# Hybrid SSD and attention block: shorter inverse roots, block 11 staged from the last scan row, slabs for the second norm taken late, a ring of 16

## The chip, the cores and the metric

One core of a Trainium2 chip runs the kernel. The engines by the names of the profile: PE multiplies matrices, DVE (vector), ACT (scalar) and POOL (GpSimd) work on tiles in on-chip memory, SP issues all transfers of this kernel, in the order of its program. The metric is the device time of one execution in microseconds, median of the runs.

## The reference, cut to what matters

The input is 1024 tokens of 1024 channels in float32. All of the following is computed once (depth 1):

```python
def rmsnorm(x, g):
    y = xf * lax.rsqrt(jnp.mean(xf * xf, axis=-1, keepdims=True) + EPS)
    return (y * g.astype(jnp.float32)).astype(x.dtype)
...
h = rmsnorm(x, norm_mix[l])
proj = h @ w_in[l]
z, xBC, dt_raw, qkv, gate_logits = jnp.split(proj, offs[1:], axis=-1)
y_ssm = mamba2_branch(z, xBC, dt_raw, ...) @ w_ssm_out[l]     # scan in chunks of 128, then a norm by 4 groups of 512 channels
y_att = dilated_attention_branch(q, k, v) ... @ w_att_out[l]  # 12 heads in 3 windows and dilations
mixed = gates[:, :, 0] * y_ssm + gates[:, :, 1] * y_att
x = x + mixed @ w_mix_out[l]
h = rmsnorm(x, norm_ffn[l])
x = x + (jax.nn.silu(h @ w_ffn_gate[l]) * (h @ w_ffn_up[l])) @ w_ffn_down[l]
return rmsnorm(x, norm_final)
```

There are thus four kinds of inverse root: the first norm, the norm of the scan's output by groups, the norm ahead of the feed-forward part (the second norm), and the final norm.

## The kernel before, in words

**Arithmetic.** Every float32 operand is split into a high and a low part, and a product is three matmuls (`mm3`). The large products go by a seven-product scheme: matrices are cut into 2 x 2 blocks, seven products of sums of blocks are formed, and added up. For the product with `w_ssm_out` the seven products have the numbers 1 to 7 and the order `SSM_ORDER` = 1, 2, 3, 6, 5, 7, 4.

**Order.** The program's order is made as the kernel is built. The matmuls are written in a main sequence; all other work is written as tasks, generators that yield what they wait for: a time, a tile, or the name of an event. A planner (`Pace`) advances a modelled clock with each matmul and runs the tasks whose conditions have come about by that clock, by priority. In `Pace.note` the model has a lag of 2.0 us for a transfer behind another transfer, dropped before the event `heads`. On the chip each engine, and SP too, works through its instructions in that order and waits on semaphores.

**Slabs.** On-chip memory is cut into slabs. `Store.room` hands them out in the order in which tasks asked, one line for all; a task that is refused waits, and those behind it wait as well.

**Inverse roots.** An inverse root is done by DVE on a tiny tile, from an integer estimate and three Newton steps. `rsqrt_steps` has 11 operations after the mean, each fed by the one before. It is called by `stat_task` (three groups of tokens in the first norm), `quarter_task` (four groups of channels in the scan) and `mo_task` (two halves of tokens, second norm). The final norm has its own form, `inverse_root`, of 14 operations, one of which (`sq`, half the argument) hangs beside the chain; `out_half` calls it for groups of 4, 1 and 3 blocks of 128 tokens. What follows is a scaling of the rows and the output transfers, six of them in the last group.

**Stages.** First norm; the projections with the scan and the attention heads as background; then the merge, in which the scan's output, scaled by rows and channels, is multiplied by `w_ssm_out`. `block_load` stages blocks of the scan's output: "11" and "21" before the merge in slabs, "12" and "22" in it in the places called `yb`; `block_task` scales them (POOL by rows, ACT by channels), `y_splits` splits them into pieces of the ring (`N_RING` slabs, 8 used by each product), `block_sums` forms the differences. Block "11" and "21" both wait for the event `heads` (the last attention head). The scan's row factors go out to `rs_d`, the last of them at the event `ssd3`.

**Attention in the merge.** `att_ops(th)` loads the attention's output of half `th` of the tokens from `att_d`, in two parts of two loads each, and splits each part: raw, high and low, three slabs while it lasts. Half 0 is asked for at product 5, half 1 in product 4, the last. `att_unit` multiplies by `w_att_out`, `x2_task` loads x anew (four loads of 512 KB for each half) and `mix_unit` multiplies by `w_mix_out`.

**Slabs held from the merge on.** 37 slabs are there at the merge. 8 hold weights, 14 the ring, 2 the gates (`gslabs`), 1 the second norm's weights (`nf`); the rest serves blocks 11 and 21, the sums (`cblk`) and `att_ops`.

Of the kernel before, what the change touches and what calls it, by code (L numbers as in the profile page):

```python
# [13 lines left out]
I32 = mybir.dt.int32  # L14
AF = mybir.ActivationFunctionType
ALU = mybir.AluOpType
# [4 lines left out]
P = 128  # L21
S = 1024
D = 1024
# [9 lines left out]
EPS = 1e-6  # L33
# [23 lines left out]
N_WTS = 7  # L57
N_WTS_B = 6
N_WTS_M = 8
N_RING = 14  # L60
N_BRIDGE = 3
N_FLAT_GATES = 4
N_SSD = 6
# [124 lines left out]
class Pace:  # L188
# [38 lines left out]
    def note(self, kind, op, aps, args, kw):  # L227
        c = self.cost(kind, op, aps, args, kw)
        outs = [_key(aps[0])] + ([_key(kw["accum_out"])] if "accum_out" in kw else [])
        ins = [_key(a) for a in aps[1:]]  # L230
        s = 0.0
        for k in ins + outs:
            t, by = self.wr.get(k, (0.0, kind))
            if by != kind or (kind == "dma" and k in ins):
                s = max(s, t)
            elif kind != "pe":
                s = max(s, t - (2.0 if kind == "dma" and "heads" in self.events else 0.025))
        for k in outs:
            t, by = self.rd.get(k, (0.0, kind))
            if by != kind:  # L240
                s = max(s, t)
        if kind == "pe":
            self.stall += max(0.0, s - self.t)
            e = self.t = max(self.t, s) + c
            lag = 0.1
        else:
            s = max(self.eng[kind], s)
            if kind == "pool" or kind == "dve" and all(_space(a) != PSUM for a in aps):
                s = self.take_port(s, c, kind)
            e = self.eng[kind] = s + c  # L250
            lag = 2.0 if kind == "dma" else 0.15
        for k in outs:
            self.wr[k] = (e + lag, kind)
        for k in ins:
            if e >= self.rd.get(k, (0.0, ""))[0]:
                self.rd[k] = (e, kind)
# [82 lines left out]
def hybrid_block(ctx, tc, x, norm_mix, w_in, b_gate, conv_w, conv_b, dt_bias, a_log, d_skip, ssm_norm,  # L339
                 w_ssm_out, w_att_out, w_mix_out, norm_ffn, w_ffn_gate, w_ffn_up, w_ffn_down, norm_final,  # L340
                 consts, rope, out):
    pace = Pace()
    nc = Core(tc.nc, pace)
# [13 lines left out]
    slabs = Store([Slot(cpool, f"slab{i}", 1024) for i in range(N_SLAB)])  # L357
# [79 lines left out]
        return w[k0 * P:(k0 + nk) * P, c0:c0 + nc_].rearrange("(k p) c -> p k c", p=P)  # L437

    def rsqrt_steps(r, v, t):
        nc.vector.tensor_scalar(t.bitcast(I32), v.bitcast(I32), 1, None, ALU.logical_shift_right)  # L440
        yield [t]
        nc.vector.tensor_scalar(r.bitcast(I32), t.bitcast(I32), -1.0, 1597463007.0, ALU.mult, ALU.add)
        yield [r]
        for _ in range(3):
            nc.vector.scalar_tensor_tensor(t, r, -0.5, r, ALU.mult, ALU.mult)
            yield [t]
            nc.vector.tensor_tensor(t, t, v, ALU.mult)
            yield [t]
            nc.vector.scalar_tensor_tensor(r, t, 1.5, r, ALU.add, ALU.mult)
            yield [r]  # L450

    def rsqrt(r, v, t):
        for _ in rsqrt_steps(r, v, t):
# [2 lines left out]
    def small(tag, w):  # L456
        return kpool.tile([P, w], F32, tag=f"{tag}{w}", name=f"{tag}{w}_{nid()}", bufs=4)
# [1247 lines left out]
    def block_load(name):  # L1705
        kh, th = BLOCKS[name]
        for i in range(4):
            kk = kh * 4 + i
            yield f"ssd{kk // 2}"
            early = name in ("11", "21")  # L1710
            if early:
                yield "heads"
                yield from spare(2)
            else:
                yield 3.0
            if kk % 2 == 0:
                yield from scale_rows(kk // 2, th, slabs if early else halves)
            if early:
                yield from slabs.room()
                blk[name].append(slabs.get([P, 2, 512]))  # L1720
            fetch_y(blk[name][i], kk, th)
            pace.fire(f"f{name}{i}")
# [65 lines left out]
    def att_ops(th):  # L1788
        ts_ = slice(th * 512, (th + 1) * 512)
        for q in range(2):  # L1790
            for i in range(2):
                yield f"sl{q * 2 + i}"
            yield from slabs.room()
            raw = slabs.get([P, 2, 512])
            for i in range(2):
                nc.sync.dma_start(raw.v[:, i, :], att_d[q * 2 + i][:, ts_])
            ysp[th, q] = yield from split_piece(raw, slabs)
            raw.free()
            pace.fire(f"ya{th}{q}")
# [44 lines left out]
    fplans = [[plan(cols_of(w, 0, KD, f * P, P), KD) for w in (w_ffn_gate, w_ffn_up)] for f in range(N_DIRECT)]  # L1844
    wstate["limit"] = len(loads)

    nf = slabs.get([P, D])
    nc.sync.dma_start(nf.v, norm_ffn[0].partition_broadcast(P))
    x2t, gst, ssq, merged, cblk, pb = {}, {}, {}, {}, {}, {}
    h2 = {"hi": [None, None], "lo": [None, None]}  # L1850

# [70 lines left out]
    def mo_task(th, cb, outs, done):  # L1922
        yield f"x2{th}"
        if cb == 0:
            ssq[th] = kpool.tile([P, 4, 2], F32, tag="ssq", name=f"ssq{th}", bufs=2)
        cs = slice(cb * 512, (cb + 1) * 512)
        for j in range(4):
            xv = x2t[th, j].v[:, cs]
            yield [outs[j], x2t[th, j]]
            nc.vector.scalar_tensor_tensor(xv, outs[j], 0.5, xv, ALU.mult, ALU.add)  # L1930
            if (j + 1) % (4 // len(done)) == 0:
                done[(j + 1) * len(done) // 4 - 1].free()
        yield from halves.room()
        junk = halves.get([P, 512])
        for j in range(4):
            t0 = th * 512 + j * P
            yield [x2t[th, j]]
            nc.sync.dma_start(x2_d[t0:t0 + P, cs], x2t[th, j].v[:, cs])
            nc.scalar.activation(junk.v, x2t[th, j].v[:, cs], AF.Square, accum_out=ssq[th][:, j, cb:cb + 1])
        junk.free()  # L1940
        if cb == 0:
            return
        for n in ("hi", "lo"):
            h2[n][th] = hp.tile([P, KD, 512], F32R, tag=f"h{n}{th}", name=f"h2{n}{th}")
        yield [ssq[th]]
        rv, rs, rt = small("rv", 4), small("rs", 4), small("rt", 4)
        nc.vector.tensor_reduce(rv, ssq[th], AX.X, ALU.add)
        nc.vector.tensor_scalar(rv, rv, 1.0 / D, EPS, ALU.mult, ALU.add)
        rsqrt(rs, rv, rt)
        raw = None  # L1950
        if th == 1:
            for n in ("T3", "T2"):
                yield from F.t_slabs(n)
            raw = F.T["T3"], F.T["T2"]
        for j in range(4):
            xj = x2t[th, j].v
            yield max(0.0, pace.rd[_key(xj)][0] - pace.t)
            nc.vector.scalar_tensor_tensor(xj, xj, rs[:, j:j + 1], nf.v, ALU.mult, ALU.mult)
            yield [xj]
            yield from split_tokens(xj, h2["hi"][th], h2["lo"][th], j * P, raw)  # L1960
            x2t[th, j].free()
            pace.fire(f"h2_{th}{j}")
        if th == 1:
            nf.free()
            slabs.pieces.extend(gslabs.pieces)

    def two_holders(t):
# [94 lines left out]
            then(kp)  # L2062
        pace.spawn(mo_task(th, cb, outs, held), 0.3, -1)

    gslabs = Store([slabs.pieces.popleft() for _ in range(2)])
    pace.fire("merge")
    for u in gates:
        u()
    for name, tag in (("T2", "hhi0"), ("12", "hlo0"), ("22", "hhi1"), ("C", "hlo1")):
        t = hp.tile([P, 4, 2, 512], F32, tag=tag, name=f"yb{name}")  # L2070
# [4 lines left out]
    for i, p in enumerate(SSM_ORDER):  # L2075
        if p == 5:
            pace.spawn(att_ops(0), 0.0, 1)
        if p == 7:
            pace.spawn(merged_place(0), 0.0, -1)
            for o in range(KD):  # L2080
                pace.spawn(gate_load(0, o))
        if p == 4:
            def then(j):
                if j == 1:
                    pace.spawn(att_ops(1), 0.0, 1)
                for o in (2 * j, 2 * j + 1):
                    att_unit(0, o)
            ssm_product(p, i % 2, then)
        else:
            ssm_product(p, i % 2)  # L2090
# [209 lines left out]

    sums = {}

    def inverse_root(v, r, t, h, sq):
        nc.vector.tensor_tensor(v, sq[:, :, 0], sq[:, :, 1], ALU.add)
        yield v
        nc.vector.tensor_scalar(v, v, EPS, None, ALU.add)
        yield v
        nc.vector.tensor_scalar(t.bitcast(I32), v.bitcast(I32), 1, None, ALU.logical_shift_right)
        nc.vector.tensor_scalar(h, v, -0.5, None, ALU.mult)
        yield t  # L2310
        nc.vector.tensor_scalar(r.bitcast(I32), t.bitcast(I32), -1.0, 1597463007.0, ALU.mult, ALU.add)
        yield r
        for _ in range(3):
            nc.vector.tensor_tensor(t, r, h, ALU.mult)
            yield t
            nc.vector.tensor_tensor(t, t, r, ALU.mult)
            yield t
            nc.vector.scalar_tensor_tensor(r, t, 1.5, r, ALU.add, ALU.mult)
            yield r

    def out_half(jj, b):

# [4 lines left out]
        s = sums[group]  # L2327
# [6 lines left out]
        s[1] -= 1  # L2334
        if s[1]:
            return
        v, r, t, h = (small(k, 4)[:, :n] for k in ("rv", "rs", "rt", "sq"))
        yield [s[0]]
        for w in inverse_root(v, r, t, h, s[0]):
            if jj < 4:  # L2340
                yield [w]
        for i in range(n):
# [79 lines left out]
```

## Time and profile before

| what | us |
|---|---|
| median of 3 runs | 2153.78 (2153.51 to 2153.95) |
| profiled execution | 2149.6 |
| its span | 2147.8 |
| PE busy | 2103.4 (98% of the span) |
| DVE busy | 1617.8 (75%) |
| ACT busy | 937.4 (44%) |
| POOL busy | 695.5 (32%) |

The profile shows one execution on the chip. The span runs from its first to its last instruction; the execution's time holds a little more around it. Busy time of PE is counted with modelled ends. The granted clock of the core is 0.994 of full speed on the mean.

### The profile page before, as it was taken

To read this page: it belongs to the slowest core of one execution; us is meant where nothing else is said; L and a number is where in the kernel's file an instruction comes from. 1 tells how busy PE (TensorE), PEld (TensorE's weight loads), DVE (VectorE), ACT (ScalarE), POOL (GpSimd) and SP (SyncE) were. 2 spreads that over 40 slices of the span, in tenths; PEclk is the share of its full clock that TensorE was granted. 3 is DMA by queue.
4 is the path that set the end of the run, shared out by engine and by line. 5 is a ranking of instruction groups with operands and counts; after the bars stand their busy time and mean duration, and the time that the engine had idled before them with its cause. 6 is when DMAs were issued, how large, how long until landed. Compare 5 with 4: busy or idle time off the path is not lost. (4 is left out here: it accounts for less than half of the span.)

```text
span 2147.8 us, 27780 instructions
## 1 busy us (share of the span) xinstructions
PE 2103.4 (98%) x10236; PEld 1736.2 (81%) x10236; DVE 1617.8 (75%) x2130; ACT 937.4 (44%) x1686; POOL 695.5 (32%) x440
## 2 busy tenths in 40 slices
PE   6999999999999999999999999999999999999997
PEld 6788888878888788878888788888878888888886
DVE  5687988877775678789784677766787777757787
ACT  4543443444434465545554543333533232324444
POOL 1333234343332445455444410002254444420102
PEclk9999999999999999999999999999999999999999
DMA  4533346655555465667548743764142323349333
GB/s 130 161 106 104 103 133 186 186 167 167 180 168 196 152 193 191 193 221 231 171 130 263 252 143 113 237 233 143 30 137 84 123 89 118 108 157 340 116 94 117
DMA packets 317707, 341.77 MB, mean 159 GB/s; under 512 B 21316, under 2 KB 251652, under 8 KB 317316
## 3 DMA queue, kind: packets, MB, share of 16 engines
q1 hardware_dynamic: 317572, 340.00, 49.8%
q8 instruction: 80, 1.31, 0.2%
q14 instruction: 55, 0.45, 0.1%
HBM read 247.02 MB, written 92.93 MB: 158 GB/s over the span
## 5 line engine op out<-in xcount | busy, mean ns | idle before, releaser
L171 POOL TENSOR_TENSOR more__5_12416<-h2hi,h2lo 128x1024 f32<-128x1024 f32 x1 | 2.4, 2390 | 238.9 <-DVE h2lo L171 238.9
L171 POOL TENSOR_TENSOR xr<-xr,nfin 128x512 f32<-128x512 f32 x12 | 17.3, 1451 | 172.0 <-ACT jk L171 172.0
L171 POOL TENSOR_TENSOR slab__10_2518<-slab__10_2518,slab__11_2519 128x1024 f32<-128x1024 f32 x12 | 32.0, 2668 | 0.0
L171 POOL TENSOR_TENSOR slab__3_5394<-slab__3_5394,slab__3_5392 128x1024 f32<-128x1024 f32 x1 | 2.4, 2400 | 53.2 <-DMA slab__3_5392<-in_rope 53.2
L171 ACT ACTIVATE jk<-xr 128x512 f32<-128x512 f32 x16 | 10.1, 633 | 16.6 <-DVE xr L171 16.6
L171 ACT ACTIVATE yb<-yb,par 128x512 f32<-128x512 f32 x16 | 10.7, 716 | 13.5 <-POOL yb L171 13.5
L171 POOL TENSOR_TENSOR slab__2_662<-slab__2_660 128x512 f32<-128x512 f32 x1 | 4.0, 3965 | 37.6 <-DMA slab__2_660<-in_w_in 37.6
L171 POOL TENSOR_TENSOR more__20_15832<-slab__17_15524,slab__43_15645 128x512 f32<-128x512 f32 x1 | 1.3, 1297 | 32.1 <-DVE slab__43_15645 L171 32.1
L171 PE MATMUL wide__1_226<-hhi,slab__1_290 128*128 128x256 f32 (+1 forms) x24 | 8.9, 369 | 2.4 <-ACT hhi L171 2.4
L171 PE MATMUL wide__1_226<-hlo,slab__1_290 128*128 128x256 f32 (+1 forms) x24 | 8.9, 371 | 2.3 <-DVE hlo L171 2.3
L171 POOL TENSOR_TENSOR slab__1_638<-hhi,hlo 128x1024 f32<-128x1024 f32 x1 | 2.4, 2410 | 27.0 <-DVE hlo L171 27.0
L171 POOL TENSOR_TENSOR slab__11_2519<-slab__11_2519,slab__10_2518 128x1024 f32<-128x1024 f32 x4 | 10.9, 2738 | 0.0
L171 POOL TENSOR_TENSOR slab__34_12811<-slab__37_12756 128x512 f32<-128x512 f32 x1 | 1.7, 1686 | 28.6 <-DVE slab__18_12765 L171 28.6
L171 POOL TENSOR_TENSOR slab__9_9887<-slab__9_9887,slab__24_9885 128x1024 f32<-128x1024 f32 x1 | 2.4, 2390 | 26.3 <-DMA slab__9_9887<-yt_d 26.3
L171 DVE TENSOR_TENSOR hlo<-slab__1_642,hhi 128x1024 fp32r<-128x1024 f32 x1 | 1.2, 1224 | 11.9 <-DMA slab__3_924<-in_w_in 11.9
L171 DVE TENSOR_TENSOR slab__28_9982<-slab__9_9887,slab__8_9981 128x1024 fp32r<-128x1024 f32 x1 | 3.3, 3260 | 8.6 <-DMA slab__29_9898<-yt_d 8.6
L171 DVE TENSOR_TENSOR slab__29_10390<-slab__37_10324,slab__39_10389 128x1024 fp32r<-128x1024 f32 x1 | 2.5, 2549 | 9.5 <-ACT slab__39_10389 L171 9.5
L171 PE MATMUL bank__1_228<-ident 128*128 128x128 f32 x36 | 6.0, 348 | 2.7 <-DMA ident<-in_consts 2.7
L171 PE MATMUL wide__37_7704<-hhi,slab__19_7581 128*128 128x512 f32 x16 | 6.9, 431 | 1.8 <-DVE slab__6_7702 L171 1.8
L171 DVE TENSOR_TENSOR slab__22_5385<-slab__21_5186,slab__13_5384 128x1024 fp32r<-128x1024 f32 x1 | 1.2, 1225 | 9.6 <-issue 9.6
L171 PEld LDWEIGHTS wide__1_226<-hlo,slab__1_290 128*128 128x128 f32 x24 | 5.3, 221 | 3.9 <-DVE hlo L171 3.8
L171 PE MATMUL wide__1_226<-hhi,slab__1_291 128*128 128x256 f32 (+1 forms) x24 | 8.3, 348 | 0.0
(8042 smaller groups left out, 8322.9 us busy)
## 6 DMA issues: line engine op xcount, KB each, us to landing
slab__11_2519<-in_w_ssm_out SPq DMA_DIRECT2D x16, 512.0 KB, 5.6
s_d<-slab__10_2518 SPq DMA_DIRECT2D x12, 512.0 KB, 4.8
slab__10_2518<-in_w_ssm_out SPq DMA_DIRECT2D x8, 512.0 KB, 6.2
yb<-yt_d SPq DMA_DIRECT2D x16, 256.0 KB, 6.2
xr<-x_d SPq DMA_DIRECT2D x8, 512.0 KB, 6.4
out<-xr SPq DMA_DIRECT2D x16, 256.0 KB, 2.3
s_d<-slab__11_2519 SPq DMA_DIRECT2D x4, 512.0 KB, 5.0
b_d<-hhi SPq DMA_DIRECT2D x1, 1024.0 KB, 5.2
```

The costliest lines, as they stand in the source:

```text
L171: r = call(*args, **kw)
```

## The change

`N_RING` goes from 14 to 16. The planner's lag for transfers behind transfers is dropped before the event `ssd3` instead of `heads`. `rsqrt_steps` has 8 operations: the integer estimate is one operation (multiply and add, no shift), followed by one step of third order and one of Newton's. `inverse_root` adds EPS in its first operation and calls `rsqrt_steps`: 9 operations. `block_load` lets block "11" wait for `ssd3`; "21" still waits for `heads`. The slabs of the gates and of the second norm's weights, and the load of these weights, move from the start of the merge to a task that is started at product 5, `late_slabs`, behind `att_ops(0)`.

```diff
-N_RING = 14
+N_RING = 16
...
-                s = max(s, t - (2.0 if kind == "dma" and "heads" in self.events else 0.025))
+                s = max(s, t - (2.0 if kind == "dma" and "ssd3" in self.events else 0.025))
...
     def rsqrt_steps(r, v, t):
-        nc.vector.tensor_scalar(t.bitcast(I32), v.bitcast(I32), 1, None, ALU.logical_shift_right)
-        yield [t]
-        nc.vector.tensor_scalar(r.bitcast(I32), t.bitcast(I32), -1.0, 1597463007.0, ALU.mult, ALU.add)
-        yield [r]
-        for _ in range(3):
-            nc.vector.scalar_tensor_tensor(t, r, -0.5, r, ALU.mult, ALU.mult)
-            yield [t]
-            nc.vector.tensor_tensor(t, t, v, ALU.mult)
-            yield [t]
-            nc.vector.scalar_tensor_tensor(r, t, 1.5, r, ALU.add, ALU.mult)
-            yield [r]
+        nc.vector.tensor_scalar(r.bitcast(I32), v.bitcast(I32), -0.5, 1597463007.0, ALU.mult, ALU.add)
+        yield r
+        nc.vector.tensor_tensor(t, r, r, ALU.mult)
+        yield t
+        nc.vector.tensor_tensor(t, t, v, ALU.mult)
+        yield t
+        nc.vector.scalar_tensor_tensor(t, t, -10.0 / 3.0, t, ALU.add, ALU.mult)
+        yield t
+        nc.vector.scalar_tensor_tensor(r, t, 5.0, r, ALU.add, ALU.mult)
+        yield r
+        nc.vector.scalar_tensor_tensor(t, r, -0.5 * 0.375 ** 3, r, ALU.mult, ALU.mult)
+        yield t
+        nc.vector.tensor_tensor(t, t, v, ALU.mult)
+        yield t
+        nc.vector.scalar_tensor_tensor(r, t, 1.5 * 0.375, r, ALU.add, ALU.mult)
+        yield r
...
             if early:
-                yield "heads"
+                yield "ssd3" if name == "11" else "heads"
                 yield from spare(2)
...
-    nf = slabs.get([P, D])
-    nc.sync.dma_start(nf.v, norm_ffn[0].partition_broadcast(P))
+    late = {}
+
+    def late_slabs():
+        for _ in range(2):
+            yield from slabs.room()
+            gslabs.pieces.append(slabs.pieces.popleft())
+        yield from slabs.room()
+        late["nf"] = slabs.get([P, D])
+        nc.sync.dma_start(late["nf"].v, norm_ffn[0].partition_broadcast(P))
...
-    gslabs = Store([slabs.pieces.popleft() for _ in range(2)])
+    gslabs = Store([])
...
         if p == 5:
             pace.spawn(att_ops(0), 0.0, 1)
+        if p == 5:
+            pace.spawn(late_slabs(), 0.0, 1)
...
-    def inverse_root(v, r, t, h, sq):
-        nc.vector.tensor_tensor(v, sq[:, :, 0], sq[:, :, 1], ALU.add)
+    def inverse_root(v, r, t, sq):
+        nc.vector.scalar_tensor_tensor(v, sq[:, :, 0], EPS, sq[:, :, 1], ALU.add, ALU.add)
         yield v
-        nc.vector.tensor_scalar(v, v, EPS, None, ALU.add)
-        yield v
-        nc.vector.tensor_scalar(t.bitcast(I32), v.bitcast(I32), 1, None, ALU.logical_shift_right)
-        nc.vector.tensor_scalar(h, v, -0.5, None, ALU.mult)
-        yield t
-        nc.vector.tensor_scalar(r.bitcast(I32), t.bitcast(I32), -1.0, 1597463007.0, ALU.mult, ALU.add)
-        yield r
-        for _ in range(3):
-            nc.vector.tensor_tensor(t, r, h, ALU.mult)
-            yield t
-            nc.vector.tensor_tensor(t, t, r, ALU.mult)
-            yield t
-            nc.vector.scalar_tensor_tensor(r, t, 1.5, r, ALU.add, ALU.mult)
-            yield r
+        yield from rsqrt_steps(r, v, t)
```

## Rows read from the trace of the kernel before

**Rows 1.** The page, busy us of each engine (share of the span) and instructions.

```profile
PE 2103.4 (98%) x10236; PEld 1736.2 (81%) x10236; DVE 1617.8 (75%) x2130; ACT 937.4 (44%) x1686; POOL 695.5 (32%) x440
```

**Rows 2.** Waits of PE: for what, us in total, times, longest us.

```profile
PE bank__3_501 L171 <- ACT slab__1_196 L171: 6.0, 1, 6.0
...
PE bank__140_10445 L171 <- DVE slab__29_10390 L171: 1.9, 1, 1.9
PE bank__142_12670 L171 <- DVE slab__13_11818 L171: 1.5, 1, 1.5
...
PE bank__140_10445 L171 <- ACT slab__39_10389 L171: 0.5, 1, 0.5
```

**Rows 3.** Timeline of ACT, first norm: start, us, operation, [idle before, releaser].

```profile
11.39 1.07 ACT L171 ACTIVATE slab__1_202<-slab__1_194 128x1024 f32<-128x1024 f32 x1 [3.45 <-DMA slab__1_194<-in_x]
...
14.44 0.56 ACT L171 CAST hhi<-bank__1_295 128x512 fp32r<-128x512 f32 x1
```

**Rows 4.** Timeline of DVE, third group of the first norm.

```profile
29.87 2.32 DVE L171 TENSOR_SCALAR rt<-rv 128x4 int32<-128x4 int32 x1
...
34.55 2.25 DVE L171 SCALAR_TENSOR_TENSOR rt<-rs 128x4 f32<-128x4 f32 x1
36.83 0.16 DVE L171 TENSOR_TENSOR rt<-rt,rv 128x4 f32<-128x4 f32 x1
...
38.21 0.16 DVE L171 SCALAR_TENSOR_TENSOR rs<-rt,rs 128x4 f32<-128x4 f32 x1
```

**Rows 5.** Timeline of POOL beside it, the last of four adds.

```profile
34.45 2.33 POOL L171 TENSOR_TENSOR slab__1_643<-hhi,hlo 128x1024 f32<-128x1024 f32 x1
```

**Rows 6.** Timeline of DVE after the last matmul, last group of the final norm.

```profile
2138.13 0.16 DVE L171 TENSOR_TENSOR rv<-osq 128x3 f32<-128x3 f32 x1 [0.85 <-ACT jk L171]
...
2140.70 0.75 DVE L171 SCALAR_TENSOR_TENSOR xr<-xr,rs,nfin 128x512 f32<-128x512 f32 x1
```

**Rows 7.** Waits of SP's queue from 1180 to 1210 us.

```profile
SPq L171 <- DMA att_d<-slab__4_9877: 5.8, 1, 5.8
```

**Rows 8.** Timeline of SP in the merge, last piece of block 21 and first `yb`.

```profile
1201.46 0.87 SPq L171 DMA_DIRECT2D slab__5_10199<-yt_d  x2
...
1206.90 1.67 SPq L171 DMA_DIRECT2D yb<-yt_d  x1
```

**Rows 9.** Timeline of ACT in the merge.

```profile
1216.79 1.34 ACT L171 ACTIVATE yb<-yb,par 128x512 f32<-128x512 f32 x2 [4.21 <-POOL yb L171]
```

**Rows 10.** Timeline of DVE in the merge.

```profile
1222.85 2.55 DVE L171 TENSOR_TENSOR slab__29_10390<-slab__37_10324,slab__39_10389 128x1024 fp32r<-128x1024 f32 x1 [9.50 <-ACT slab__39_10389 L171]
```

**Rows 11.** Timeline of SP, last scan row and first piece of block 11.

```profile
1143.19 0.29 SPq L171 DMA_DIRECT2D rs_d<-half__21_9789  x1
...
1150.07 1.35 SPq L171 DMA_DIRECT2D slab__9_9887<-yt_d  x2
```

**Rows 12.** Timeline of SP, second attention load, first and last x load.

```profile
1363.21 0.90 SPq L171 DMA_DIRECT2D slab__6_11411<-att_d  x2
...
1377.56 0.33 SPq L171 DMA_DIRECT2D slab__32_11563<-in_x  x1
...
1381.28 0.42 SPq L171 DMA_DIRECT2D slab__32_11569<-in_x  x1
```

**Rows 13.** DMA issues from 1345 to 1390: KB each, median us to landing.

```profile
slab__6_11411<-att_d SPq DMA_DIRECT2D x2, 256.0 KB, 4.5
...
slab__32_11569<-in_x SPq DMA_DIRECT2D x1, 512.0 KB, 6.2
```

**Rows 14.** Timeline of ACT, cast of the second attention load.

```profile
1374.72 1.05 ACT L171 CAST slab__15_11552<-slab__6_11411 128x1024 fp32r<-128x1024 f32 x1
```

**Rows 15.** Timeline of DVE, its subtraction.

```profile
1379.18 1.22 DVE L171 TENSOR_TENSOR slab__32_11553<-slab__6_11411,slab__15_11552 128x1024 fp32r<-128x1024 f32 x1
```

**Rows 16.** Timeline of PE, its first matmul.

```profile
1386.02 0.39 PE L171 MATMUL wide__49_11623<-slab__15_11552,slab__40_11588 128*128 128x512 f32 x1
```

More of the change, by code (lines that the diff above doesn't have):

```diff
@@ L1957, in mo_task @@
             yield max(0.0, pace.rd[_key(xj)][0] - pace.t)
-            nc.vector.scalar_tensor_tensor(xj, xj, rs[:, j:j + 1], nf.v, ALU.mult, ALU.mult)
+            nc.vector.scalar_tensor_tensor(xj, xj, rs[:, j:j + 1], late["nf"].v, ALU.mult, ALU.mult)
             yield [xj]
@@ L1963, in mo_task @@
         if th == 1:
-            nf.free()
+            late["nf"].free()
             slabs.pieces.extend(gslabs.pieces)
@@ L2336, in out_half @@
             return
-        v, r, t, h = (small(k, 4)[:, :n] for k in ("rv", "rs", "rt", "sq"))
+        v, r, t = (small(k, 4)[:, :n] for k in ("rv", "rs", "rt"))
         yield [s[0]]
-        for w in inverse_root(v, r, t, h, s[0]):
+        for w in inverse_root(v, r, t, s[0]):
             if jj < 4:
```

## The prediction

> **What bounds the kernel now.** I read the page's busy times first: PE, the matmul engine, is busy for 2103.4 of the 2147.8 us of the span [rows 1], and the strip of granted clock on the page shows nines throughout. A kernel in that state becomes faster only where PE stands still, or by doing fewer matmuls. The change removes no matmul, so the sum below is a sum over gaps of PE. Span less busy time is 44.4 us. The list of PE's waits says whom it waited for: the longest by far is 6.0 us in the first norm, for a tile that ACT scales; 1.9 and 0.5 us stand together at the start of the merge; 1.5 us stand at the second norm [rows 2]. The last chain of small operations, after the last matmul, is no wait of PE, and the timeline of DVE shows it [rows 6].
>
> The sum is made against the profiled execution: 2149.6 us, which is the span of 2147.8 and 1.8 around it. The median of the three runs, 2153.78, lies 4.2 us above; I carry differences over unchanged.
>
> **First norm, the shorter root.** `rsqrt_steps` goes from 11 operations to 8, three less. A step between such operations without disturbance is (38.21 - 36.83) / 7 = 0.197 us [rows 4]. In the third group of the first norm they are not all so: three take 2.3 us, and each ends with one of POOL's adds (34.55 + 2.25 = 36.80, and the add 34.45 + 2.33 = 36.78) [rows 4, 5]. DVE is held there while POOL adds, whatever the operation is. After the change three operations still stand beside those three adds, now the integer one and two of the products; what is saved is only from the undisturbed end, 8 operations there becoming 5: 3 x 0.197 = 0.59 us. The scaled tile that ends PE's 6.0 us waits for the end of this chain, so I put **-0.59** on the path. The other end is the mean: 11 operations from 29.87 to 38.37 are 0.77 each, three by that mean would be -2.3; that would need the saved operations to be the held ones, and they can't be, since the adds aren't shortened.
>
> The Trainium skill ("SBUF — State Buffer", Who interferes with whom) says that a DVE operation with one input in SBUF, outside of the modes that use both port pairs, doesn't contend with GpSimd, and one with two does. By it the first operation after the change, which has one input, would slip through in 0.2 us, the next three be held, and four be left: 0.2 us more saved. The row of the int32 operation with one input that took 2.32 us [rows 4] speaks against that for this shape.
>
> The first group of this norm gains nothing: PE's first operand, `hhi`, is cast by ACT at 14.44 us, behind the `ACTIVATE` that waited for an x tile until 11.39 [rows 3]; DVE's shorter chain ends earlier beside that transfer. If the transfer were no cover it would be another -0.59. The second group stands under matmuls of the first, and no PE wait of it is in the list: between 0 and -0.59, I take **-0.2**, near the end that the rows speak for. The four roots of the scan and the first of the two after the merge end no wait of PE: 0. The second one's gap of 1.5 us [rows 2] waits on the order of the transposes rather than on the root; 0 to -0.59, taken as 0.
>
> **Tail.** `inverse_root` goes from 14 operations to 9. The one named `sq` hangs beside the chain and costs nothing. So 13 links become 9; a link is (2140.70 - 2138.13) / 13 = 0.198 us [rows 6]; 4 links are **-0.79**. Nothing covers it: ACT and SP wait for the result, and the output transfers shift as a whole. With five links it would be -0.98.
>
> **Merge: slabs and block 21.** At the merge two slabs were set aside for gates and one for the second norm's weights; these three are now taken only at product 5, and the ring takes two more. One slab net is free before product 5, two fewer after it. In the trace of before the last piece of block 21 is issued at 1201.46 [rows 8], after SP had waited 5.8 us for a slab whose old contents were still going out to `att_d` [rows 7]. SP issues in order, so the `yb` pieces queued behind came only at 1206.90 [rows 8]; ACT's scaling of them stood idle 4.2 us for POOL [rows 9], the subtraction of DVE came 9.5 us after its last work and took 2.55 [rows 10], and PE lost 0.5 + 1.9 us [rows 2]. With one more slab that very piece needn't reuse the slab in question; `yb` comes up to 5.8 us earlier, and the 2.4 us go. But the two additional ring pieces ask for slabs in the same line, and the wait could come back under another name. Bounds: -2.4 (all gone) to +1.9 (a second gap like the longer one). I take **-2.0**.
>
> Block 11 is staged from the last scan row on: that row leaves at 1143.19 and the block's first piece goes at 1150.07 [rows 11], so the loads move 6 us ahead. PE uses the block only in the merge, some 50 us later: 0. They pass the queue of SP in front of the last heads' transfers; should one of those be late, it costs at most those 6 us of cover, and I see no PE wait there. The event that the planner's lag rule looks for moves too; it changes modelled times alone, so only the order. Different orders elsewhere: ±1.5, as large as the single gaps that stand in the list.
>
> **Attention operand after product 4.** This gives time back. `att_ops(1)` needs three slabs for each half. Two slabs fewer means that only two are free when it starts, and it must wait until the first half's operands go or the ring is given up. Its second load, issued at 1363.21 before, then comes at about 1377.6, where the four x loads start [rows 12]. In front of these it would land 4.5 us later [rows 13], at 1382.1 to 1383.0; the cast takes 1.05 [rows 14], the subtraction 1.22 [rows 15]: the first operand is there at about 1384.1, or 1385 behind another cast, the second at 1386.2. PE reads it from 1386.02 on [rows 16]. So 0 to +0.4; I take **+0.4**. The Trainium skill ("DMA: Bandwidth & Descriptors", Anatomy of one DMA — SWDGE (gpsimd) path) fits a transfer as 2.0 us and its bytes over 436 GB/s, 2.6 us for 256 KB, fitted on GpSimd's own path. By that the term would be 0; the rows here show 4.5.
>
> Sum: -0.59 - 0.2 - 0.79 - 2.0 + 0.4 = **-3.2 us**: 2146.4 in the profile, 2150.6 as a median.
>
> **Rivals.**
> *The merge wait only moves* (the ring or the held slab takes the new one): -0.59 - 0.2 - 0.79 + 0.4 = -1.2, **2152.6**. For it: the line for slabs is in order, and the net gain is one slab. Against it: only one piece was late.
> *All of it goes*: -0.59 - 0.59 - 0.98 - 2.4 - 0.59 (second norm), no give-back: -5.15, **2148.6**. For it: each is a wait or chain that shortens. Against it: it needs every upper end.
> *The second attention half comes behind the x loads* (slower). The last x load is issued at 1381.28 and takes 0.42 [rows 12]; the two pieces are issued by 1382.1, land 4.5 to 6.2 us later [rows 13], by 1388.3, cast and subtraction end by 1390.6, and PE, which wants the second operand at 1386.25 (one matmul after 1386.02), stands up to 4.4 us. In place of +0.4 this gives -3.6 + 4.4 = +0.8, **2154.6**; with the merge's wait left, 2156.6. It decides from a landing after about 1384.0 (1386.25 - 1.22 - 1.05). For it: x2's loads are queued at just this time. Against it: its request stands ahead of theirs in the line.
>
> **Numbers.** Forecast 0.45, moved merge wait 0.20, all 0.17, late attention 0.18. Of no change one can tell 0.2%, 4.3 us (2149.5 to 2158.1). Below it: 0.28 of the forecast's share (it reaches from 2148.4 to 2152.6 by the order's ±1.5 and the merge's end), most of "all", and little else: 0.31. Above it: a quarter of the late attention and a share for orders gone wrong: 0.10. Between: 0.59. The range of 8 in 10 is 2147.6 to 2155.8.
>
> **What would show it.** In the first norm: five operations of 0.16 after the last held one, PE's gap 5.4 instead of 6.0. At the end: 1.8 us from `rv` to the scaling instead of 2.57. In the merge: no SP wait for `att_d` ahead of block 21, and the two PE waits gone; if they stand under another name, the second case holds. After product 4: the second `att_d` load beside the x loads, and a PE wait for its operand if it is late. The prediction is wrong if gaps of several us appear in the scan or the FFN, where nothing but order changes, or if PE's busy time moves by more than 2 us.

## The result and the profile after

The changed kernel is slower by 0.2%: ratio 1.0020 (95% interval 1.0014 to 1.0026), 2155.24 us as a median of 20 runs against 2151.45 of 20 runs of the kernel before. The time lies in the predicted range (2147.6 to 2155.8), but that is luck: the range was set around 2153.78, the median of before at that time, and as a difference it reached from -6.2 to +2.0 us. Measured are +3.8 us, where -3.2 were forecast: the sign is the wrong one. In the profiled executions the span goes from 2147.8 to 2152.5 us.

The page after, busy us of each engine, to be held against [rows 1]:

```profile
PE 2106.1 (98%) x10236; PEld 1737.0 (81%) x10236; DVE 1614.1 (75%) x2088; ACT 936.7 (44%) x1686; POOL 690.0 (32%) x440
```

DVE does 42 instructions less; PE, with the same matmuls, is busy 2.7 us longer. Where the rest is shows in the waits of PE (for what, us in total, times, longest), to be held against [rows 2]:

```profile
PE bank__3_492 L171 <- ACT slab__1_196 L171: 5.5, 1, 5.5
...
PE wide__39_8401 L171 <- DVE slab__28_8369 L171: 2.9, 1, 2.9
...
PE bank__109_8328 L171 <- ACT half__15_8246 L171: 2.4, 1, 2.4
...
PE bank__134_10422 L171 <- DVE slab__29_10365 L171: 2.0, 1, 2.0
PE bank__154_12637 L171 <- DVE slab__45_11797 L171: 1.8, 1, 1.8
PE wide__46_10584 L171 <- DVE slab__29_10538 L171: 1.7, 1, 1.7
...
PE wide__46_10263 L171 <- ACT more__1_10256 L171: 1.0, 1, 1.0
PE bank__106_8371 L171 <- ACT half__17_8358 L171: 1.0, 1, 1.0
```

The 6.0 us of the first norm became 5.5, as forecast. But two places are new: 2.9, 2.4 and 1.0 us between 984 and 999 us, in the scan, where the forecast had nothing; and 2.0, 1.7 and 1.0 in the merge, where it had seen a gap go. Adding up all gaps of PE by stretch (worked out from the two traces; a gap is the time between the end of one matmul and the start of the next, and the first row includes the 2.7 us ahead of the first matmul):

| stretch, us | before | after | difference |
|---|---|---|---|
| to 100, first norm | 17.6 | 14.8 | -2.8 |
| 100 to 960 | 7.5 | 5.8 | -1.7 |
| 960 to 1010, scan | 0.2 | 6.4 | +6.2 |
| 1200 to 1300, merge | 2.5 | 5.2 | +2.7 |
| 1350 to 1450, attention operand, mix | 0.0 | 1.4 | +1.4 |
| 1450 to 1600, second norm, FFN | 5.1 | 2.2 | -3.0 |
| sum of gaps | 33.1 | 35.9 | +2.8 |

Gaps +2.8, PE's busy time +2.7, and after the last matmul 11.26 to 10.48, -0.8: together the 4.7 us of the span. These are single executions, one of each kernel.

**Who waits in the scan.** Waits of ACT in the changed kernel from 960 to 1000 us, and its timeline at the end of the longest:

```profile
ACT slab__7_8269 L171 <- DMA att_d<-slab__6_7987: 13.5, 1, 13.5
```

```profile
983.97 2.02 ACT L171 COPY slab__7_8269<-wide__38_8025 64x1024 f32<-64x1024 f32 x2 [13.54 <-DMA att_d<-slab__6_7987]
986.02 0.59 ACT L171 COPY half__15_8246<-bank__108_8273 128x512 f32<-128x512 f32 x1
```

The store itself, in SP's timeline:

```profile
974.22 0.73 SPq L171 DMA_DIRECT2D att_d<-slab__6_7987  x1
```

`slab__6` and `slab__7` are the sixth and seventh use of one and the same slab. `slot_bg` issues the store of 512 KB at 974.22 and frees the slab in the program right behind it; the planner gives it to ACT's copy, which can only start at 983.97, 9.75 us after the issue. The copy in the next line, of `half__15`, is the one that PE's 2.4 us gap names. The 2.9 us hang on the same slab by way of DVE, which stood still for that copy too and then worked with one pause of 1.07 us up to the sum that PE's gap names:

```profile
986.03 1.23 DVE L171 TENSOR_TENSOR wide__38_8025<-wide__38_8025,slab__3_5381 128x1024 f32<-128x1024 f32 x1 [7.69 <-ACT slab__7_8269 L171]
...
996.98 1.97 DVE L171 TENSOR_TENSOR slab__28_8369<-wide__38_8025,slab__7_8269 128x1024 f32<-128x1024 f32 x1
```

The 1.0 us in between was not followed back. In the kernel before the same store is there, and the slab's next user is a load, so SP waits for it, from 970 to 990 us (the wait, then SP's timeline):

```profile
SPq L171 <- DMA att_d<-slab__6_8017: 9.1, 1, 9.1
```

```profile
974.85 0.51 SPq L171 DMA_DIRECT2D att_d<-slab__6_8017  x1
984.54 0.32 SPq L171 DMA_DIRECT2D slab__7_8262<-v_d  x1
```

The load comes 9.69 us after the store's issue, and the gaps of PE from 960 to 1010 us are 0.2 us in all. The duration of the store is thus much the same; what changed is who has been given the slab. The Trainium skill ("DMA: Bandwidth & Descriptors", Anatomy of one DMA — SWDGE (gpsimd) path) has a fit of 2.0 us and bytes over 436 GB/s, for GpSimd's own path; by it the store would have ended after an estimated 3.2 us. The rows show about three times that, at a DMA share of 0.98 from 972 to 984 us; the measurement decides.

**Clock.** The windows of the changed kernel around the first of these gaps (stretch, length, busy time of PE, PEld, DVE, ACT, POOL; granted clock, DMA share, GB/s):

```profile
980.00:987.00 7.00, 4.61 (x22) 3.53 (x21) 0.97 (x1) 2.60 (x3) 0.93 (x1) 1.00 0.61 212
987.00:991.00 4.00, 4.00 (x19) 3.67 (x18) 3.97 (x8) 0.99 (x4) 4.00 (x3) 0.57 0.00 0
991.00:997.00 6.00, 3.96 (x20) 2.46 (x18) 4.93 (x6) 5.42 (x12) 4.04 (x3) 1.00 0.63 208
```

After standing still for 2.4 us PE has a granted clock of 0.57 for the next 4 us, most of it at the level of 1.2 GHz. The kernel before shows the same behind its merge gap: 0.85 and 0.69 in the two stretches up to 1230 us, then 1.00:

```profile
1222.30:1226.50 4.20, 1.86 (x6) 1.16 (x6) 3.65 (x2) 4.20 (x6) 4.20 (x2) 0.85 0.01 3
1226.50:1230.00 3.50, 3.50 (x12) 2.77 (x11) 3.50 (x3) 3.50 (x6) 1.14 (x1) 0.69 0.91 271
1230.00:1234.00 4.00, 4.00 (x19) 3.30 (x18) 4.00 (x4) 1.93 (x3) 1.67 (x1) 1.00 0.96 307
```

A gap can cost its length and the slow matmuls behind it. As a whole, though, the clock does not explain the 2.7 us more of PE's busy time: by the records of the granted clock (worked out from the two traces) each kernel has 17.1 us at 1.2 GHz up to its last matmul, before also behind its 2.2 us gap at 714, and PE is busy in 13.9 of them before and in 15.0 after. Where the rest of the 2.7 us lies was not found.

**The shorter chains.** DVE, third group of the first norm, and the last group of the final norm, both after, against [rows 4] and [rows 6]:

```profile
29.93 2.32 DVE L171 TENSOR_SCALAR rs<-rv 128x4 int32<-128x4 int32 x1
32.29 2.29 DVE L171 TENSOR_TENSOR rt<-rs 128x4 f32<-128x4 f32 x1
34.61 2.26 DVE L171 TENSOR_TENSOR rt<-rt,rv 128x4 f32<-128x4 f32 x1
36.91 0.16 DVE L171 SCALAR_TENSOR_TENSOR rt<-rt 128x4 f32<-128x4 f32 x1
...
2143.58 0.16 DVE L171 SCALAR_TENSOR_TENSOR rv<-osq 128x3 f32<-128x3 f32 x1 [0.85 <-ACT jk L171]
...
2145.35 2.08 DVE L171 SCALAR_TENSOR_TENSOR xr<-xr,rs,nfin 128x512 f32<-128x512 f32 x3
```

Three operations are still held by POOL, for 2.3 us each, and five short ones follow; the end takes 1.77 us instead of 2.57.

**The merge.** Waits of SP from 1190 to 1225 us after, against [rows 7]:

```profile
SPq L171 <- ACT more__1_10256 L171: 5.9, 1, 5.9
SPq L171 <- ACT more__1_10187 L171: 4.7, 1, 4.7
```

The wait for `att_d` ahead of block 21 is gone, and two waits for gate tiles of ACT stand there.

One thing stands the wrong way round ahead of the prediction: by the code the planner's lag of 2.0 us for a transfer behind a transfer is dropped from the event on, not before it.

### The profile page after: what moved, and what is told of

It is laid out like the page before. It is cut to its first block, busy times and chain, and to the rows that moved or that the text cites. A ratio compares the mean times of both kernels' runs of the same rounds, so it can differ in the third digit from the quotient of the medians.

```text
span 2152.5 us, 27751 instructions
## 1 busy us (share of the span) xinstructions
PE 2106.1 (98%) x10236; PEld 1737.0 (81%) x10236; DVE 1614.1 (75%) x2088; ACT 936.7 (44%) x1686; POOL 690.0 (32%) x440
## 4 chain that ended last, share of the span: by engine, by line
PE 80%; DVE 8%; DMA 5%; ACT 3%; issue 2%; POOL 1%; SPq 1%; DVEq 0%; POOLq 0%; ACTq 0%
SPq L171 1%; PE wide__57_16966 L171 1%; PE wide__56_16965 L171 1%; PE wide__56_16516 L171 1%; PE wide__55_16515 L171 1%; PE wide__55_16028 L171 1%; PE wide__54_16027 L171 1%; DMA yb<-yt_d 1%; PE wide__39_8401 L171 1%; PE wide__40_8988 L171 1%; PE wide__32_5770 L171 1%; PE wide__37_7681 L171 1%; PE wide__37_7857 L171 1%; PE wide__33_6220 L171 1%; PE wide__42_9689 L171 1%
## 5 line engine op out<-in xcount | busy, mean ns | idle before, releaser
L171 POOL TENSOR_TENSOR xr<-xr,nfin 128x512 f32<-128x512 f32 x12 | 17.3, 1450 | 172.0 <-ACT jk L171 172.0
L171 DVE TENSOR_TENSOR hlo<-slab__1_633,hhi 128x1024 fp32r<-128x1024 f32 x1 | 1.2, 1225 | 11.8 <-ACT hhi L171 11.8
L171 POOL TENSOR_TENSOR yb<-yb,last__1_10290 128x1024 f32<-128x1024 f32 x2 | 4.8, 2393 | 14.3 <-DMA yb<-yt_d 14.3
L171 PEld LDWEIGHTS wide__1_226<-hhi,slab__1_286 128*128 128x128 f32 x24 | 5.8, 240 | 4.4 <-ACT hhi L171 4.2
```

Of the source, the lines that this page charges most:

```text
L171: r = call(*args, **kw)
```

## Experiments

Theory A: the short root of the scan, worth nothing on the chip, shifts the planner's clock, and the new order gives ACT the slab of a running store. Theory B: the short root itself gains nothing on the chip. Theory C: the loss is the staging. Sixteen runs, each compared with the kernel before in runs on the same chip. They are judged by the ratio and by PE's gaps in three places (us, worked out from one trace of each):

| run | ratio to before (95%) | 960 to 1010 | merge | 1550 to 1600 |
|---|---|---|---|---|
| before | 1 | 0.2 | 2.5 | 2.7 |
| changed | 1.0020 (1.0014 to 1.0026) | 6.4 | 5.2 | 0.4 |
| e1 roots, old order | 1.0001 (0.9992 to 1.0010) | 0.0 | 1.9 | 2.8 |
| e2 roots, new order | 1.0005 (0.9995 to 1.0015) | 6.2 | 2.5 | 0.4 |
| e3 staging | 0.9990 (0.9981 to 0.9998) | 0.6 | 1.1 | 2.6 |
| e4 all, old order | 0.9978 (0.9968 to 0.9988) | 0.6 | 0.5 | 2.8 |
| e5 changed, slab held | 0.9977 (0.9968 to 0.9986) | 1.2 | 3.9 | 0.4 |
| e6 late slabs | 0.9985 (0.9976 to 0.9994) | 0.0 | 0.0 | 2.7 |
| e7 late slabs, ring 16 | 1.0005 (0.9995 to 1.0014) | 0.9 | 6.1 | 2.7 |
| e8 block 11 | 1.0006 (0.9996 to 1.0016) | 0.4 | 3.2 | 2.8 |
| e9 scan root | 1.0027 (1.0017 to 1.0038) | 7.5 | 3.2 | 2.8 |
| e10 e7, slab held | 1.0060 (1.0047 to 1.0072) | 2.4 | 11.4 | 2.7 |
| e11 late slabs, roots, old order | 0.9981 (0.9971 to 0.9991) | 0.3 | 0.7 | 2.9 |
| e12 e11 and block 11 | 0.9974 (0.9964 to 0.9984) | 0.3 | 0.0 | 2.8 |
| e13 changed, ring 14 | 0.9998 (0.9988 to 1.0007) | 6.2 | 0.4 | 0.4 |
| e14 e5, ring 14 | 0.9958 (0.9946 to 0.9969) | 1.4 | 0.0 | 0.4 |
| e15 e12, norm 2 seen | 0.9957 (0.9944 to 0.9970) | 0.5 | 0.0 | 0.5 |
| e16 e11, norm 2 seen | 0.9965 (0.9954 to 0.9977) | 0.2 | 1.4 | 0.4 |

Two of the traces are not typical of their runs: e7's is of the slowest of 11 (2156.61 us, median 2151.76), e13's of the fastest of 12 (2145.82, median 2151.37).

**Roots or staging, and is it the order?** In e1 and e4 the eight short operations are issued past the planner, which notes the eleven old ones:

```diff
     def rsqrt(r, v, t):
-        for _ in rsqrt_steps(r, v, t):
-            pass
+        dve = nc.vector.real
+        dve.tensor_scalar(r.bitcast(I32), v.bitcast(I32), -0.5, 1597463007.0, ALU.mult, ALU.add)
...
+        for op, aps in (("tensor_scalar", [t, v]), ("tensor_scalar", [r, t]),
+                        *(("scalar_tensor_tensor", [t, r, r]), ("tensor_tensor", [t, t, v]),
+                          ("scalar_tensor_tensor", [r, t, r])) * 3):
+            pace.note("dve", op, aps, (), {})
```

e2 is the change's `rsqrt_steps` and `inverse_root` alone, e3 all the rest of its diff.

> The kernel before with both short inverse roots, but the planner is charged with the 11 operations as before, so that PE, ACT, POOL and SP get their instructions in the order of before. Theory A (a shorter root moves the planner's clock, and the time is lost to the new order it writes): no gap of several us near 985 us, first norm 0.5 us less, chain at the end 0.8 us less, in all 1.3 us faster than before (ratio 0.9994). Theory B (the short root itself is slower on the chip, or its saved time is given back by what follows at once): no faster than before, or slower.

> The kernel before with both short inverse roots and nothing else, the planner seeing them. Theory A: the three PE gaps of 6.3 us in all at 984 to 999 us stand here too, ACT's copy waiting for the store att_d; the scan up to 975 us is 3.6 us earlier than before; up to 1010 us it is 2.7 us later; the end 0.8 us shorter; in all 1.5 to 3 us slower than before. Theory C (the loss is the staging: ring, late slabs, block 11): no such gap, 1.3 us faster than before.

> The ring of 16, block 11 from the last scan row, the late slabs and the planner's event, with the old inverse roots. Theory A: nothing changes up to 1143 us; in the merge PE loses 2 to 3 us more than before (about 5 instead of 2.3 us of gaps between 1205 and 1260), 0.6 us more after product 4; 2 to 3 us slower than before. Theory C with the whole loss here: 4 us slower or more. Prediction's theory (a slab more removes the wait in the merge): 2 us faster.

> All parts of the change, but the planner charged with 11 operations for the short root, so that the order up to the merge is that of before and then that of the staging alone. Theory A: e3 less 1.3 us, and without the 6.3 us at 984 to 999: faster than the changed kernel by 3 to 4 us. Theory C: as slow as the changed kernel.

The same short roots give no gap at 984 in the old order and 6.2 us of gaps in the new one; e2's ACT waits there for the same store:

```profile
ACT slab__7_8269 L171 <- DMA att_d<-slab__6_7987: 13.3, 1, 13.3
```

Theory C falls: the staging alone is not slower (0.9990, 1.8 us less by the medians, about what the prediction's theory said for e3), and theory A's expectation for e3, slower, was wrong with it. By the gaps at 984 theory A held in e1, e2 and e4. e1's gain, 0.06% expected, is below what its interval tells, so its time does not rule out theory B; its trace has the shorter wait in the first norm (5.45 us) and the shorter end (10.48). e2's gaps are clear, its time isn't (1.0005, the gap after the second norm gone in exchange). e4, all of the change with the old root's durations in the planner, is 0.42% under the changed kernel by the ratios (0.9978 / 1.0020), more than the 3 to 4 us expected. Against before it gains 4.7 us by the ratio (2.6 to 6.9), 3.5 by the medians: with the old order kept up to the merge, this interval holds the 3.2 us of the forecast.

**Which root, and is it that slab?** e9 has the short root in `quarter_task` alone. e5 is the changed kernel with one line more:

```diff
         nc.sync.dma_start(att_d[slot], us[0].v)
+        yield 12.0
         us[0].free()
```

> Before, with the short root only in quarter_task (the four norms of the scan's groups), where no wait of PE hangs on it; the planner sees it. Theory A (it is the planner's shifted clock, and it is this use that shifts it): ACT's copy waits 10 us or more for the store att_d, PE gaps of 5 to 6.5 us between 980 and 1000 us, and no gain at either end: 5 to 8 us later than before by 1010 us, slower than before. Rival (the first norm's shorter roots shift the order): order and time of before, no such gap.

> The changed kernel, but the task that stores a slot of attention (slot_bg) keeps its slab for 12 us of the planner's clock after it has issued the store to att_d, so that ACT's copy is not given this slab while the store still runs. Theory A (the 6.3 us at 984 to 999 come from that one slab): ACT no longer waits 13.5 us for att_d there, these gaps shrink to under 1.5 us, 6 us or more of the loss gone up to 1010 us; the merge is written anew and open within 3 us either way; 2 to 8 us faster than the changed kernel. Rival (the place is late anyway, DVE is full there): another wait of 4 us or more in the same place, no gain.

e9 does nothing but take three operations of 0.2 us out of four chains off the path, and is the slower by 0.27%. Its PE and ACT waits in the place:

```profile
PE bank__109_8337 L171 <- ACT half__15_8255 L171: 3.5, 1, 3.5
PE wide__39_8410 L171 <- DVE slab__28_8378 L171: 2.9, 1, 2.9
PE bank__106_8380 L171 <- ACT half__17_8367 L171: 1.0, 1, 1.0
```

```profile
ACT slab__7_8278 L171 <- DMA att_d<-slab__6_7996: 14.6, 1, 14.6
```

In e5 a single PE wait is left there, for a load, and the kernel comes out 0.43% under the changed one by the ratios:

```profile
PE bank__109_8314 L171 <- DMA slab__26_8228<-bc_d: 1.2, 1, 1.2
```

The held slab changes the order behind it too, so not every us of that is the slab's; the gaps of the place are.

**What the staging's parts do.** e6: only `late_slabs`. e7: the same and `N_RING = 16`. e8: only the lines of `block_load` and `Pace.note`. e10: e7 with the line of e5.

> Before, with only the gates' slabs and the second norm's weights taken at product 5. Prediction's mechanism (three more slabs free at the merge, block 21 doesn't wait for the store of att_d): no SP wait for att_d ahead of block 21, the 2.3 us of PE gaps at 1222 and the lower clock behind them gone, 3 us faster than before. Rival (the late slabs matter only with the larger ring or the early block 11): gap of 1.5 us or more stays, same as before.

> As the run with the late slabs alone, and the ring of 16. Prediction's mechanism: one slab more than before is enough, same as late slabs alone within 1 us, 2.5 to 3.5 us faster than before. Rival (the ring takes the slabs back): the gaps in the merge are those of before, no faster.

> Before, with only block 11 staged from the last scan row and the planner's event moved with it. Prediction (hidden, 0): the gaps in the merge within 1 us of before, time same as before. Rival (the early block is what frees SP's queue in the merge): 2 us or more faster; or, as SP's queue then holds the last heads' loads back, slower with a new PE gap before 1200 us.

> The kernel with late slabs and the ring of 16, and the slab of an att_d store kept for 12 us of the planner's clock, as in the changed kernel with the slab held. Theory A (the 6.1 us gap at 1201 us of the run with the ring of 16 is the same fault, a slab handed to ACT while its store runs): no ACT wait for att_d there, gap under 2 us, 4 us or more faster than that run. Rival (the larger ring starves block 21): gap of 4 us or more stays.

The late slabs alone do what the prediction said: no gap in the merge. From PE's 6000th matmul (1181.8 us) to its 6400th the run gains 4.9 us on before, 2.5 of gaps and 2.4 of faster matmuls: the lower clock behind the gap of before (0.85 and 0.69 above) isn't there. Block 11 alone is the same as before. The ring of 16 undoes the gain, in e7 through ACT again:

```profile
ACT slab__5_10211 L171 <- DMA att_d<-slab__4_9877: 14.6, 1, 14.6
```

```profile
PE wide__45_10262 L171 <- ACT slab__5_10211 L171: 6.1, 1, 6.1
```

Here ACT's gate tile was given a slab whose store was under way. Holding that slab (e10) took the wait for `att_d` away, as expected, but the gap, which was expected to go too, stayed: ACT now waits 9.4 and 8.0 us for DVE at two other slabs, and PE 7.7 us. Theory A in its narrow form (it is the store) falls for this place; that the ring's two slabs are lacking fits both runs. It is not so in every order: e3 and e4 have the ring of 16 too, with block 11 early, and 1.1 and 0.5 us of gaps in the merge.

**Without the ring; adding up.** e11: late slabs and short roots, planner charged with 11 operations. e12: the same with block 11 early. e13: the changed kernel with `N_RING = 14`. e14: that with the line of e5. e15 and e16: e12 and e11, with the planner seeing the short root in `mo_task`.

> Before, with the late slabs and both short roots, the planner charged with 11 operations: ring of 14, block 11 as before. Theory A: no merge gap as with the late slabs alone (some 4.9 us with the low clock behind it), 0.5 us at the start, 0.8 us at the end: 5 us faster than before, ratio 0.9975. Rival (the parts don't add up): no faster than the late slabs alone.

> As the run with late slabs and short roots in the order of before, and block 11 from the last scan row. Theory A: block 11 early is hidden and worth 0, so the same time within 1 us. Rival (early staging takes the slabs that block 21 needs, or frees SP): more than 2 us apart from that run, with a new gap or one less between 1180 and 1260 us.

> The changed kernel with the ring of 14. Theory A1 (the two slabs of the larger ring are what the merge lacks in the changed order): the gaps at 984 to 999 stay as they are, the 5.1 us of gaps between 1205 and 1260 shrink to under 2 us, 3 us faster than the changed kernel. Rival A2 (in the changed order the merge's stalls come from the order itself, whatever the ring): gaps in the merge of 4 us or more, no faster.

> The changed kernel with the stored slab held for 12 us and the ring of 14. Theory A1: as the held one with the ring of 16, less its 3.9 us of gaps in the merge: 0.2 to 0.3% under before plus another 2 to 4 us. Rival A2: merge as with the ring of 16 or another gap of 3 us or more.

> Late slabs, block 11 early, short roots everywhere, ring of 14; the planner sees the short root only in the second norm (mo_task) and is charged with 11 operations in the first norm and the scan. Theory N (the 2.5 us gap at 1565, gone in the changed kernel, goes because the planner sees the second norm's shorter root): this gap goes here too, and the run is 2 to 3 us faster than the same kernel with no root seen. Rival (it goes because of the other order from the scan on): the gap stays, same time.

> The same without the early block 11: late slabs, short roots, ring of 14, the planner seeing the root of the second norm alone. Theory N: the gap at 1565 goes, no gap in the merge, 6 to 8 us faster than before (ratio 0.9965). Rival: gap stays, as with no root seen (ratio 0.998).

e11 and e12 are not told apart from each other by time, nor e11 from e6. e13 decides for A1: in the changed order too, the merge's 5.2 us become 0.4 with a ring of 14, and the 6.2 in the scan stay; by the ratios it is 0.22% under the changed kernel. e14 takes those away as well and is 0.42% faster than before. e4 and e12 differ in the ring alone and are not told apart (0.9978 and 0.9974): what the ring of 16 costs hangs on the order it meets. In e15 and e16 the 2.6 us gap at 1565 is gone, which stands in e11 and e12: it goes as soon as the planner sees the second norm's shorter root, whatever came before. e16 keeps 1.4 us of gaps in the merge, where none was expected. e14 and e15 (2140.94 and 2142.77 us against 2150.94) beat both kernels by the same amount; neither has the ring of 16. Why a seen root of the second norm helps and a seen one in the scan harms, the runs do not show; what exactly it moved at 1565 I did not trace.

## Why the prediction was wrong

The step that failed is the scan's: "the four roots of the scan ... end no wait of PE: 0". That they are off PE's path is right, but their length is an input of the planner, and I bounded "different orders elsewhere" by ±1.5, as large as single gaps of the old list. The new order opened 6.2 us in one place, more with the low clock behind it, and made the merge worse as well (5.2 us of gaps with the ring of 16, where e3 has 1.1 and e4 0.5 with the same ring). A gap of the old trace is no bound for an order that has not run. The prediction's own signs of being wrong both came: gaps of several us in the scan, and PE's busy time moved by more than 2 us (2.7).

Point by point:
- First norm, -0.59: PE's 6.0 became 5.5 (6.04 to 5.47 in the timeline). Right, and every trace shows it: 6.04 to 6.06 in the seven with the old root there, 5.45 to 5.47 in the eleven with the short one. What PE keeps of it one pair of traces can't tell: its 200th matmul starts 0.51 earlier (47.96 to 47.44), but traces with the same root differ by 1.7 us (old) and 2.3 us (short) there; over all of them the short root is 0.8 us earlier on the mean. The first group's transposes come 1.35 earlier in this pair (11.69 to 10.34), which I had at nothing; PE then waits longer for `hhi` (2.05 to 2.79) and has a granted clock of 0.50 instead of 0.61 from 16 to 20 us. The held integer operation took 2.32 us again. The prediction's 0.2 us for an operation that slips through leave out their own condition, outside of the modes that use both port pairs; no row shows in which mode this operation ran.
- Tail, -0.79: measured -0.80. Right.
- Merge, -2.0: the mechanism is right (e6), the size too small, since I counted the gap and not the slow matmuls behind it: 4.9. But the sum had it with the ring's two slabs, as "one slab net". That slab was nearly enough in the order of e3 and e4 (3.5 and 3.6 us gained over the same 400 matmuls), and not in the changed order (1.4 us lost there; e13 against the changed kernel), nor in e7. The rival "the merge wait only moves", at 0.20, is what happened, and it named the ring; it should have had more, and a worse price than zero.
- Block 11, 0: right alone, within e8's interval. Beside the ring of 16 it isn't shown to be nothing: e3 is e7 with block 11 early, and has 1.1 us of gaps in the merge for e7's 6.1 (by the ratios 0.15% less; the intervals touch).
- Attention operand, +0.4: the second load did move, from its place long before the x loads [rows 12] to just ahead of them:

```profile
1384.09 0.81 SPq L171 DMA_DIRECT2D slab__31_11528<-att_d  x2
1385.44 0.33 SPq L171 DMA_DIRECT2D more__3_11540<-in_x  x1
```

  PE waits 0.6 for its operand at 1392.67. Right; the rival of 4.4 us did not come. The prediction's own times gave only 0.2 (1386.2 less 1386.02), so that 0.4 lay nearer is luck, and in e4, where the load is just ahead of the x loads too, PE doesn't wait for it.
- Second norm, 0: its gap at 1521 stays (1.5 to 1.8); the one of 2.5 at 1565 goes, 2.1 us that no term had. The prediction named only the 1.5; the list of before has the larger one too:

```profile
PE bank__154_13045 L171 <- DVE slab__16_12875 L171: 2.5, 1, 2.5
```

The slower side came by a mechanism that none of the rivals named.

## What to carry to other kernels

Where a program writes the order from modelled durations, any edit of a duration is an edit of the whole order behind it: try it with the old durations kept, and the edit's own worth and the order's come apart. Look in the trace for stalls that the old order hides on an idle queue, such as a slab reused while its store still runs: the next order may put a busy engine there. Price a PE gap with the slow matmuls that can follow it, and add a buffer only after asking who else stands in the line for the memory.

## What the runs showed of the hardware

A 512 KB store from the chip's memory took 9.75 us from its issue to the start of its slab's next user in the changed kernel, and 9.69 before. A PE gap of 2.3 us lay in a stretch of 4.2 us with a granted clock of 0.85, and the 3.5 us behind that stretch had 0.69 (windows of before from 1222.3 on), but not each gap does this: behind the 2.5 us at 1565 the window from 1565 to 1575 of the kernel before has 1.00. Behind the same gap e6 has 0.60 from 1564.7 to 1569. Of the eleven traces that have this gap, at 2.4 to 2.6 us, five show a stretch at 1.2 GHz behind it and six don't (worked out from the traces), so one trace doesn't tell what a gap of this length costs.
